# Stick-breaking attention: scores of two heads from half arrays, and the meta tokens' sums over both key blocks at once

## The chip, the cores and the metric

The kernel runs as one program on one core of a Trainium2 chip. The metric is the device time of one execution in microseconds (us). The median of three runs of the kernel before is 1894.74 us (1891.46 to 1902.87).

## The reference, cut to what matters

The network is one block with sparse attention and a mixture of 32 experts, and a second block with two layers. The change lies in the first layer of the second block, the stick-breaking attention over 272 positions (16 meta tokens, then 256 tokens), 16 heads of 64.

```python
def _sb_block(q_blk, k, v, q_pos):
    ...
    z = jnp.einsum('bhqd,bhkd->bhqk', q_blk, k).astype(jnp.float32) * (SB_HEAD_DIM ** -0.5)
    ...
```

From the scores z (masked to keys before the query) each key gets log sigmoid(z) minus the sum of softplus(z) over the keys that lie between it and the query; the exponential of that is the weight of its value row. So for every query the kernel needs, beside z and softplus(z), running sums of softplus(z) over the keys above each key.

## The kernel before, in words

The first block and the experts take the first 1224 us of the span. Then come the attention of this case (1224 to 1405 us), a dense MLP, a recurrent layer, and a last dense MLP. Dense products are split: each fp32 operand is the sum of a high and a low part, and `mm3` (L290 to L292) issues three products of 272 columns for each 128 x 128 tile of weights. The high part of the weights is cast by ScalarE (L190), the low part subtracted by GpSimd or VectorE (L192).

The attention is laid between the dense products of the query, key and value projections. The heads are taken two at a time, as pair t (0 to 7): the two heads lie on partitions 0 to 63 and 64 to 127 of `qT`, `kT` and `vT`. `sb_steps(t)` gives a list of (step, function); `steps` puts it into a background list, and `fill` runs one entry after every second chunk of a dense product (six products). Pairs come in twos, `PAIR` = 11 entries apart, after each group of three projections. Every engine works off its own instructions in the program's order, so the list is the order on all of them.

For a pair, keys are in three parts: "b" (the second 128 tokens), "a" (the first 128 tokens) and "m" (the 16 meta tokens of both heads, 32 rows). The functions are:

- `meta` (step 0): GpSimd lays the meta tokens' keys and values of both heads into padded tiles `km` and `vm`.
- `scores("b")` and `scores("a")` (steps 2 and 3): both heads' scores by one product over all 128 partitions. This needs queries that are zero outside their head: `qz` holds 2 x 272 columns, and `ev_q` fills it with two GpSimd copies (L1973, L1974) from `qT`. A bf16 product with the identity adds the causal mask (L1857, L1860).
- `soft`, `plus`, `rest`: ScalarE does Abs, Exp, Ln on z and copies z to `w`; VectorE forms softplus `sp`; ScalarE casts its high part `sh`, and VectorE subtracts to get the low part `sl` (L1850).
- `sum_b`, `sum_a`, `sum_m` (steps 7, 9, 11): products with triangles and rows of minus ones give the running sums; `weights` adds them to `w` and takes the exponential.
- `values` (step 13): the product with the values, split into `o_hi` and `o_lo`.

In `sum_m` the meta tokens' sum over all later keys is made of `sh` and `sl` of part "a" (256 columns each) and of the unsplit fp32 softplus of part "b" (128 columns, L1903), for each head apart.

Of the kernel before, what the change touches and what calls it, by code (L numbers as in the profile page):

```python
# [8 lines left out]
F32 = mybir.dt.float32  # L9
F32R = mybir.dt.float32r  # L10
# [4 lines left out]
ALU = mybir.AluOpType  # L15
# [6 lines left out]
META = 16  # L22
NT = META + S
# [220 lines left out]
class Ker:  # L244
# [1544 lines left out]
    def sb_steps(self, t):  # L1789
        nc = self.nc  # L1790
        qz, kT, vT = self.qz[t], self.kT[t], self.vT[t]
        sa = self.sba
        st = {}
# [21 lines left out]
        def bank(x):  # L1815
            shape, p = parts[x]
            z = self.ps_o.tile(shape, F32, name="z" + x, tag="z" + x, bufs=1)
            z = st["z" + x] = z[:p]
            st["f" + x] = z if x == "m" else z.rearrange("p a b -> p (a b)")
            return z  # L1820

        def soft(x):

            shape, p = parts[x]
            z = st["f" + x]
            l = sa.tile([128, z.shape[1]], F32, name="l" + x, tag="l" + x)[:p]
            s = sa.tile([128, z.shape[1]], F32, name="sp" + x, tag="sp" + x)[:p]
# [3 lines left out]
            w = st["w" + x] = sa.tile([128, z.shape[1]], F32, name="w" + x, tag="w" + x, bufs=2)[:p]  # L1831
            if x != "a":
                nc.scalar.copy(out=w, in_=z)
            st["p" + x] = l, s

        def plus(x):

            shape, p = parts[x]
            z, (l, s) = st["f" + x], st["p" + x]
            nc.vector.scalar_tensor_tensor(out=s, in0=z, scalar=0.0, in1=l, op0=ALU.max, op1=ALU.add)  # L1840
            s = st["s" + x] = s if x == "m" else s.rearrange("p (a b) -> p a b", a=2)
            hi = st["h" + x] = sa.tile(shape, F32R, name="sh" + x, tag="sh" + x)[:p]
            nc.scalar.copy(out=hi, in_=s)

        def rest(x):
            shape, p = parts[x]
            lo = st["l" + x] = sa.tile(shape, F32R, name="sl" + x, tag="sl" + x)[:p]
            if x == "a":
                nc.vector.tensor_copy(out=st["wa"], in_=st["fa"])
            nc.vector.tensor_tensor(out=lo, in0=st["s" + x], in1=st["h" + x].bitcast(F32), op=ALU.subtract)  # L1850

        def scores(x):
            mk = self.maskd.unsqueeze(1).to_broadcast([128, 2, 128])
            z = bank(x)
            if x == "b":
                mm(z, lhsT=kT[:, META + 128:NT], rhs=qz[:, :, META + 128:NT], start=True, stop=False)
                mm(z, lhsT=self.identb, rhs=mk, start=False, stop=True)  # L1857
            elif x == "a":
                mm(z, lhsT=kT[:, META:META + 128], rhs=qz[:, :, META:NT], start=True, stop=False)  # L1859
                mm(z[:, :, 0:128], lhsT=self.identb, rhs=mk, start=False, stop=True)  # L1860
            else:
                mm(z, lhsT=st["km"], rhs=self.qT[t], start=True, stop=False)
                mm(z[:, 0:16], lhsT=self.identb[0:32, 0:32], rhs=self.maskm[0:32], start=False, stop=True)
            soft(x)

        def weights(x, sums):

            shape, p = parts[x]
# [4 lines left out]
            st["w" + x] = w if x == "m" else w.rearrange("p (a b) -> p a b", a=2)  # L1873

        def sum_b():
            def sums(c):
                for x in ("hb", "lb"):
                    mm(c[:, 0:256].rearrange("p (a b) -> p a b", a=2), lhsT=self.negtri, rhs=st[x], start=(x == "hb"),
                       stop=(x == "lb"))
                return c[:, 0:256]  # L1880

            weights("b", sums)

        def sum_a():
            def sums(c):
# [5 lines left out]
                return c  # L1891
# [17 lines left out]
        def values():  # L1909
            v, wa, wb, wm = st["v"], st["wa"], st["wb"], st["wm"]  # L1910
            ot = self.ps_m.tile([128, 512], F32, name="ot", tag="ss", bufs=1)[:, 0:NT]
            for a in range(2):
# [10 lines left out]
                (8, lambda: plus("m")), (9, sum_a), (9, lambda: rest("m")), (11, sum_m), (13, values)]  # L1923
# [16 lines left out]
    def post_layer0(self, h):  # L1940
        nc = self.nc
        with ExitStack() as ctx:
# [13 lines left out]
            self.qz, self.kT, self.vT, self.qT = {}, {}, {}, {}  # L1956
# [10 lines left out]
            def ev_q(g):  # L1967
                def evac(m, ps):
                    t = 2 * g + m
                    qz = qzs[t % 4]  # L1970
# [4 lines left out]
                    self.qz[t], self.qT[t] = qz, qT  # L1975
# [295 lines left out]
```

## Time and profile before

| what | value |
|---|---|
| median of three runs | 1894.74 us |
| the profiled execution | 1895.64 us |
| its span on the core | 1893.8 us |
| TensorE busy | 1776.0 us, 94% of the span |
| VectorE, ScalarE, GpSimd busy | 991.1, 632.8, 410.2 us |
| read from memory | 546.83 MB, 289 GB/s over the span |

The span is the time on the core; the execution's own time lies 1.84 us above it. Busy time of TensorE overlaps itself, since products are pipelined: a product of 272 columns is shown as 0.29 us long, and the next one starts 0.125 us after it. So what a product costs is read from one start to the next, not from its length.

### The profile page before, as it was taken

The page shows a single profiled execution, that of the slowest core. Times are in us where ns is not written, and L with a number is a line of the kernel's source. Part 1 is how long each engine was busy: PE and PEld are TensorE (multiplying, and loading weights), DVE is VectorE, ACT ScalarE, POOL GpSimd, SP SyncE. Part 2 cuts the span into 40 slices and gives each one's busy share as a digit, 9 for nine tenths or more (in the row PEclk, how much of TensorE's full clock was granted, in tenths as well). Part 3 has the DMA queues.
Part 4 walks back from the last instruction along what each step waited for, and adds up shares of the span by engine and source line. Part 5 has one row for each costly group of instructions (what it writes and reads, how often), then busy time and mean ns, then how long its engine had stood idle before and what let it go on. Part 6 is the DMA issues. An engine that isn't in the chain of part 4 may idle for free. (4 is left out here: it accounts for less than half of the span.)

```text
span 1893.8 us, 25887 instructions
## 1 busy us (share of the span) xinstructions
PE 1776.0 (94%) x10035; PEld 1107.9 (58%) x10035; DVE 991.1 (52%) x1617; ACT 632.8 (33%) x1110; POOL 410.2 (22%) x269
## 2 busy tenths in 40 slices
PE   3988779999999999999999999799999999889998
PEld 2866643333334343333434333377779999889986
DVE  7686744544444433444443444545566543996622
ACT  3444322111211101121110112346565544756633
POOL 4533310000000000000000000164433344554443
PEclk6999989999999999999999999899999999999999
DMA  9544789999999999999999999552245545346552
GB/s 342 205 149 135 251 326 370 424 425 424 424 425 423 425 425 401 424 424 425 423 426 424 400 424 424 222 175 74 74 134 175 182 157 178 112 128 181 181 188 79
DMA packets 183342, 549.60 MB, mean 290 GB/s; under 512 B 8656, under 2 KB 101968, under 8 KB 150256
## 3 DMA queue, kind: packets, MB, share of 16 engines
q1 hardware_dynamic: 182592, 545.99, 74.5%
q0 software_dynamic: 432, 1.57, 0.3%
q8 instruction: 80, 1.31, 0.3%
q10 hardware_dynamic: 192, 0.35, 0.1%
q14 instruction: 46, 0.38, 0.1%
HBM read 546.83 MB, written 1.05 MB: 289 GB/s over the span
## 5 line engine op out<-in xcount | busy, mean ns | idle before, releaser
L192 POOL TENSOR_TENSOR wsp<-wraw,wsp 128x1024 fp32r<-128x1024 f32 x137 | 337.1, 2465 | 1383.8 <-PE cb L1568 964.6
L190 ACT CAST wsp<-wraw 128x1024 fp32r<-128x1024 f32 x208 | 215.4, 1044 | 108.8 <-PE f L2184 46.9
L290 PE MATMUL dps<-hn_hi,wsp 128*128 128x272 f32 (+1 forms) x816 | 242.8, 297 | 9.5 <-DVE h L1935 4.1
L291 PE MATMUL dps<-hn_lo,wsp 128*128 128x272 f32 (+1 forms) x816 | 237.1, 291 | 4.0 <-DVE hn_lo L1637 4.0
L292 PE MATMUL dps<-hn_hi,wsp 128*128 128x272 f32 (+1 forms) x816 | 237.4, 291 | 0.8 <-DVE wsp L192 0.8
L1572 DVE SCALAR_TENSOR_TENSOR h<-cb,vec,h 128x256 f32<-128x256 f32 x256 | 111.8, 479 | 227.5 <-PE cb L1568 227.5
L1441 PE MATMUL u<-wraw_s,xs 128*64 128x512 f32 x728 | 208.5, 602 | 0.9 <-DVE gl L1471 0.9
L1469 ACT COPY gl<-u 64x512 f32<-64x512 f32 x120 | 66.8, 583 | 418.0 <-PE u L1441 357.0
L1441 PE MATMUL u<-wraw,xs 128*64 128x512 f32 x648 | 195.2, 604 | 0.0
L290 PEld LDWEIGHTS dps<-hn_hi,wsp 128*128 128x128 f32 x816 | 157.4, 193 | 14.7 <-issue 5.8
L1441 PE MATMUL u<-wraw_r,xs 128*64 128x512 f32 x544 | 164.4, 608 | 0.0
L291 PEld LDWEIGHTS dps<-hn_lo,wsp 128*128 128x128 f32 x816 | 157.3, 193 | 5.4 <-DVE hn_lo L1637 4.7
L292 PEld LDWEIGHTS dps<-hn_hi,wsp 128*128 128x128 f32 x816 | 157.3, 193 | 1.1 <-DVE wsp L192 1.1
L1471 DVE TENSOR_TENSOR gl<-u,gl 64x512 f32<-64x512 f32 x120 | 79.1, 680 | 140.9 <-ACT gl L1469 140.9
L192 DVE TENSOR_TENSOR wsp<-wraw,wsp 128x1024 fp32r<-128x1024 f32 x71 | 91.2, 1287 | 90.6 <-ACT wsp L190 90.5
L1441 PEld LDWEIGHTS u<-wraw_s,xs 128*64 128x64 f32 x728 | 54.7, 136 | 75.4 <-issue 66.2
L2035 DVE TENSOR_TENSOR y<-r 128x272 f32<-128x272 f32 (+1 forms) x64 | 53.5, 835 | 62.6 <-ACT r L2032 62.6
L1441 PEld LDWEIGHTS u<-wraw,xs 128*64 128x64 f32 x648 | 49.5, 136 | 60.4 <-issue 51.5
L1543 PE MATMUL y<-wraw_s,at 128*64 128x512 f32 x368 | 82.8, 594 | 0.0
L1543 PE MATMUL y<-wraw_r,at 128*64 128x512 f32 x336 | 78.0, 605 | 3.7 <-SPq L1246 3.7
L1567 PE MATMUL cb<-st,y 128*128 128x256 f32 x256 | 80.2, 336 | 0.1
L1510 ACT COPY at<-at_ps 128x512 f32<-128x512 f32 x34 | 19.9, 587 | 176.9 <-PE at_ps L1508 176.9
(514 smaller groups left out, 3325.4 us busy)
## 6 DMA issues: line engine op xcount, KB each, us to landing
wraw_s<-in_exp_w SPq DMA_DIRECT2D x147, 1024.0 KB, 14.3
wraw_r<-in_exp_w SPq DMA_DIRECT2D x120, 1024.0 KB, 15.4
wraw<-in_exp_w SPq DMA_DIRECT2D x117, 1024.0 KB, 14.1
wraw<-in_mlp_w_up SPq DMA_DIRECT2D x32, 1024.0 KB, 5.4
wraw<-in_mlp_w_down SPq DMA_DIRECT2D x32, 1024.0 KB, 4.8
wraw<-in_ada_w SPq DMA_DIRECT2D x18, 1024.0 KB, 5.9
wraw<-in_sb_w_qkv SPq DMA_DIRECT2D x12, 1024.0 KB, 4.9
wraw<-in_lru_w_in SPq DMA_DIRECT2D x8, 1024.0 KB, 5.0
```

The lines of the kernel that those rows point to most:

```text
L190: nc.scalar.copy(out=hv, in_=src)
L192: e.tensor_tensor(out=lv, in0=src, in1=lr, op=ALU.subtract)
L290: mm(o, lhsT=wh, rhs=xh, start=first, stop=False)
L291: mm(o, lhsT=wh, rhs=xl, start=False, stop=False)
L292: mm(o, lhsT=wl, rhs=xh, start=False, stop=last)
L1441: mm(u[n][64 * j:64 * j + 64], lhsT=xs[:, k, o:o + 64], rhs=w[:, ns], start=(q == 0), stop=(q == 3))
L1469: nc.scalar.copy(out=o, in_=u[n][64:128])
L1471: nc.vector.tensor_tensor(out=o, in0=u[n][R], in1=o, op=ALU.add)
L1543: mm(y[n][64 * j:64 * j + 64], lhsT=at[:, k, 0:64], rhs=w[:, ws], start=(q == 0), stop=(q == 3))
L1567: mm(o, lhsT=yh[:, m * 128:m * 128 + 128], rhs=st, start=True, stop=False)
L1572: nc.vector.scalar_tensor_tensor(out=h[:, m, META:NT], in0=o, scalar=self.mod[:, 40 + m:41 + m], in1=h[:, m, META:NT], op0=ALU.mult, op1=A ...
L2035: nc.vector.tensor_tensor(out=y[:, :n], in0=r[:, :n], in1=r[:, :n], op=ALU.mult)
```

## The change

The padded queries `qz`, their four memsets and the two GpSimd copies per pair go. Scores "b" and "a" are made by two products each, one per head, on 64 of the 128 partitions, straight from `qT` and `kT`. Both parts lie in one tile `z` of two banks, a bank for each head: columns 0 to 255 are part "a", columns 256 to 383 part "b". The mask is added per head. For `sum_m`, GpSimd adds softplus "b" into the later half of softplus "a" (in place, after VectorE has taken `sl` of it), ScalarE casts the result to `ch`, GpSimd subtracts to get `cl`, and the meta tokens' sums take `ch` and `cl` over 256 columns; the fp32 products are gone. The new function `both` stands at step 8, ahead of `plus("m")`.

```diff
         def bank(x):
+            if x == "m":
+                z = self.ps_o.tile([128, NT], F32, name="zm", tag="zm", bufs=1)[:32]
+            else:
+                if x == "b":
+                    st["z"] = self.ps_o.tile([128, 2, 512], F32, name="z", tag="z", bufs=1)
+                z = st["z"][:, :, 0:256] if x == "a" else st["z"][:, :, 256:384]
+            st["f" + x] = z
+            return z
...
         def rest(x):
...
             nc.vector.tensor_tensor(out=lo, in0=st["s" + x], in1=st["h" + x].bitcast(F32), op=ALU.subtract)
+            if x == "a":
+                s = st["sa"]
+                nc.gpsimd.tensor_tensor(out=s[:, :, 128:256], in0=s[:, :, 128:256], in1=st["sb"], op=ALU.add)
+
+        def both():
+            hi, lo = tiles("a", "ch", "cl", dt=F32R)
+            nc.scalar.copy(out=hi, in_=st["sa"])
+            nc.gpsimd.tensor_tensor(out=lo, in0=st["sa"], in1=hi.bitcast(F32), op=ALU.subtract)
+            st["hc"], st["lc"] = hi, lo
...
         def scores(x):
-            mk = self.maskd.unsqueeze(1).to_broadcast([128, 2, 128])
             z = bank(x)
-            if x == "b":
-                mm(z, lhsT=kT[:, META + 128:NT], rhs=qz[:, :, META + 128:NT], start=True, stop=False)
-                mm(z, lhsT=self.identb, rhs=mk, start=False, stop=True)
-            elif x == "a":
-                mm(z, lhsT=kT[:, META:META + 128], rhs=qz[:, :, META:NT], start=True, stop=False)
-                mm(z[:, :, 0:128], lhsT=self.identb, rhs=mk, start=False, stop=True)
+            if x == "m":
...
             else:
+                o = META + 128 if x == "b" else META
+                for a in range(2):
+                    hs = slice(64 * a, 64 * a + 64)
+                    mm(z[:, a], lhsT=kT[hs, o:o + 128], rhs=qT[hs, o:NT], start=True, stop=False)
+                for a in range(2):
+                    mm(z[:, a, 0:128], lhsT=self.identb, rhs=self.maskd, start=False, stop=True)
...
         def sum_m():
...
                 for a in range(2):
                     cs = slice(16 - 16 * a, 48 - 16 * a)
-                    mm(z[:, 16:NT], lhsT=self.negselr[:, cs], rhs=st["ha"][:, a], start=False, stop=False)
-                    mm(z[:, 16:NT], lhsT=self.negselr[:, cs], rhs=st["la"][:, a], start=False, stop=False)
-                    mm(z[:, 144:NT], lhsT=self.c("negsel")[:, cs], rhs=st["sb"][:, a], start=False, stop=False)
+                    for x in ("hc", "lc"):
+                        mm(z[:, 16:NT], lhsT=self.negselr[:, cs], rhs=st[x][:, a], start=False, stop=False)
                 mm(z, lhsT=self.negtrim[0:32], rhs=st["lm"], start=False, stop=True)
...
-                (8, lambda: plus("m")), (9, sum_a), (9, lambda: rest("m")), (11, sum_m), (13, values)]
+                (8, both), (8, lambda: plus("m")), (9, sum_a), (9, lambda: rest("m")), (11, sum_m), (13, values)]
...
-            qzs = [sa.tile([128, 2, NT], F32, name=f"qz{i}") for i in range(4)]
-            for q in qzs:
-                nc.gpsimd.memset(q, 0.0)
...
                     nc.vector.scalar_tensor_tensor(out=qT, in0=ps, scalar=0.125, in1=f["rs"], op0=ALU.mult, op1=ALU.mult)
-                    nc.gpsimd.tensor_copy(out=qz[0:64, 0], in_=qT[0:64])
-                    nc.gpsimd.tensor_copy(out=qz[64:128, 1], in_=qT[64:128])
```

The change moves instructions at three places. The names in square brackets are the semaphores that an instruction waits for; a wait that an earlier instruction of the engine has already made is not repeated.

TensorE, the two score products of a pair (t = 2), before and then in the change; z, za and zb are the scores, dps is a dense product:

```order
L1856 MATMUL zb<-qz_7892,kT 128x256
L1857 LDWEIGHTS identb
L1857 MATMUL zb<-maskd_c,identb 128x256
L290 MATMUL dps<-hn_hi,wsp 128x272
L291 MATMUL dps<-hn_lo,wsp 128x272
L292 MATMUL dps<-hn_hi,wsp 128x272
L290 MATMUL dps<-hn_hi,wsp 128x272
L291 MATMUL dps<-hn_lo,wsp 128x272
L292 MATMUL dps<-hn_hi,wsp 128x272
L1859 MATMUL za<-qz_7892,kT 128x512
L1860 LDWEIGHTS identb
L1860 MATMUL za<-maskd_c,identb 128x2x128
```

```order
L1880 MATMUL z<-maskd_c,identb 128x128
L290 MATMUL dps<-hn_hi,wsp 128x272
L291 MATMUL dps<-hn_lo,wsp 128x272
L292 MATMUL dps<-hn_hi,wsp 128x272
L290 MATMUL dps<-hn_hi,wsp 128x272
L291 MATMUL dps<-hn_lo,wsp 128x272
L292 MATMUL dps<-hn_hi,wsp 128x272
L1878 MATMUL z<-qT,kT 128x256 [waits Activation_49]
L1878 MATMUL z<-qT,kT 128x256
L1880 LDWEIGHTS identb
L1880 MATMUL z<-maskd_c,identb 128x128
```

The six dense products between the two scores are the same; the first product of part "a" (L1878, 128x256) now waits for ScalarE, where L1859 waited for nothing of its own. The ScalarE instruction whose count it waits for is the copy of part "b" out of `z` into `wb`, the fourth of the four that `soft("b")` issues; both parts lie in the same two banks.

TensorE, the meta tokens' sums (t = 2), before and then in the change; sh, sl, ch, cl are the high and low parts:

```order
L1898 MATMUL sum<-shm,negtrim_c 32x272 [waits DVE_49,Activation_49]
L1901 MATMUL sum<-sha,negselr 32x256
L1902 MATMUL sum<-sla,negselr 32x256
L1903 MATMUL sum<-spb,cst 32x128
L1901 MATMUL sum<-sha,negselr 32x256
L1902 MATMUL sum<-sla,negselr 32x256
L1903 MATMUL sum<-spb,cst 32x128
L1904 MATMUL sum<-slm,negtrim_c 32x272 [waits DVE_49]
```

```order
L1913 MATMUL sum<-shm,negtrim_c 32x272 [waits DVE_49,Activation_49]
L1917 MATMUL sum<-cha,negselr 32x256
L1917 MATMUL sum<-cla,negselr 32x256 [waits Pool_49]
L1917 MATMUL sum<-cha,negselr 32x256
L1917 MATMUL sum<-cla,negselr 32x256
L1918 MATMUL sum<-slm,negtrim_c 32x272 [waits DVE_49]
```

The two fp32 products (L1903) are gone, and the third product waits for GpSimd's `cla`.

GpSimd, from the end of `meta` of pair 0 to that of pair 1, before and then in the change; wsp is a low part of weights:

```order
L1804 COPY vm<-vT 64x16
L1973 COPY qz_7892<-qT 64x272 [waits DVE_49]
L1974 COPY qz_7892<-qT 64x272
L192 TENSOR_TENSOR wsp<-wraw,wsp 128x1024 [waits PE_49,Activation_49,Pool_49]
L1973 COPY qz_7893<-qT 64x272 [waits DVE_49]
L1974 COPY qz_7893<-qT 64x272 [waits Pool_49]
L192 TENSOR_TENSOR wsp<-wraw,wsp 128x1024 [waits DMAHW1_49,Activation_49,Pool_49]
L1802 MEMSET km 128x32
```

```order
L1804 COPY vm<-vT 64x16
L192 TENSOR_TENSOR wsp<-wraw,wsp 128x1024 [waits PE_49,Activation_49,Pool_49]
L1861 TENSOR_TENSOR spa<-spa,spb 128x2x128 [waits DVE_49]
L192 TENSOR_TENSOR wsp<-wraw,wsp 128x1024 [waits DMAHW1_49,Activation_49]
L1866 TENSOR_TENSOR cla<-spa,cha 128x512 [waits Activation_49]
L1802 MEMSET km 128x32
```

The copies to `qz` are gone. The addition (L1861) and the subtraction (L1866) stand on either side of a piece of weights (L192); so it is in pairs 0, 2 and 4. In pairs 1, 3, 5, 6 and 7 the subtraction follows the addition at once.

## Rows read from the trace of the kernel before

**Rows 1.** The page, busy tenths of TensorE in 40 slices of 47.3 us.

```profile
PE   3988779999999999999999999799999999889998
```

**Rows 2.** Stages of the window view (engines' busy time, granted clock PEclk, DMA share, GB/s).

```profile
1262.00:1265.00 3.00, 3.00 (x12) 1.87 (x11) 0.46 (x1) 1.68 (x4) 2.09 (x1) 0.50 0.00 0
1280.00:1320.00 40.00, 37.64 (x254) 30.58 (x254) 21.05 (x39) 24.29 (x51) 20.20 (x23) 1.00 0.20 67
1406.00:1408.00 2.00, 2.00 (x11) 2.00 (x10) 1.99 (x6) 1.73 (x4) 0.00 (x0) 0.50 0.96 264
```

**Rows 3.** TensorE's waits from 1250 to 1410 us: total, times, longest.

```profile
PE vtr L1810 <- POOL vm L1804: 3.2, 1, 3.2
PE dps L290 <- DVE h L1935: 2.8, 2, 2.1
PE sum L1878 <- DVE slb L1850: 2.8, 2, 1.4
PE sum L1904 <- DVE slm L1850: 1.6, 2, 0.8
```

**Rows 4.** Timeline, the scores of pair 2 (start, length, engine, line).

```profile
1291.93 0.59 PE L1856 MATMUL zb<-qz,kT 128*128 128x256 f32 x2
1292.36 0.27 PE L1857 MATMUL zb<-maskd_c,identb 128*128 128x256 bf16 x1
1293.22 1.02 PE L1859 MATMUL za<-qz,kT 128*128 128x512 f32 x2
1293.86 0.35 ACT L1833 COPY wb<-zb 128x256 f32<-128x256 f32 x1
1294.08 0.27 PE L1860 MATMUL za<-maskd_c,identb 128*128 128x256 bf16 x1
```

**Rows 5.** Timeline, scores of two heads in the first block.

```profile
134.44 0.93 PE L834 MATMUL sc<-z 64*128 64x128 f32 x8
135.29 0.39 PE L290 MATMUL dps<-hh,wsp 128*128 128x256 f32 x1
```

**Rows 6.** Timeline, part "a" and the meta tokens' sums of pair 7.

```profile
1386.60 0.68 DVE L1850 TENSOR_TENSOR sla<-spa,sha 128x512 fp32r<-128x512 f32 x1
...
1389.27 0.31 PE L1898 MATMUL sum<-shm,negtrim_c 32*32 32x272 f32 x1
1389.50 0.31 PE L1901 MATMUL sum<-sha,negselr 128*32 128x256 f32 x1
1389.65 0.28 PE L1902 MATMUL sum<-sla,negselr 128*32 128x256 f32 x1
1389.86 0.41 PE L1903 MATMUL sum<-spb,cst 128*32 128x128 f32 x2
...
1390.88 0.31 PE L1904 MATMUL sum<-slm,negtrim_c 32*32 32x272 f32 x1
```

**Rows 7.** Timeline, the same place in pair 2.

```profile
1300.66 0.62 ACT L1843 CAST sha<-spa 128x512 fp32r<-128x512 f32 x1 [3.10 <-DVE spa L1840]
...
1301.48 0.68 DVE L1850 TENSOR_TENSOR sla<-spa,sha 128x512 fp32r<-128x512 f32 x1
...
1302.99 1.04 ACT L190 CAST wsp<-wraw 128x1024 fp32r<-128x1024 f32 x1
...
1304.16 2.36 POOL L192 TENSOR_TENSOR wsp<-wraw,wsp 128x1024 fp32r<-128x1024 f32 x1 [0.71 <-POOL qz L1974]
...
1304.38 2.43 DVE L1850 TENSOR_TENSOR slm<-spm,shm 32x272 fp32r<-32x272 f32 x1 [0.56 <-ACT shm L1843]
...
1306.87 0.31 PE L1904 MATMUL sum<-slm,negtrim_c 32*32 32x272 f32 x1 [0.79 <-DVE slm L1850]
```

**Rows 8.** Timeline, GpSimd and ScalarE ahead of pair 0.

```profile
1231.15 0.85 POOL L1656 TENSOR_TENSOR sq<-sq 128x272 f32<-128x272 f32 x1
...
1244.97 1.99 ACT L190 CAST wsp<-wraw 128x1024 fp32r<-128x1024 f32 x2
...
1247.56 11.76 POOL L192 TENSOR_TENSOR wsp<-wraw,wsp 128x1024 fp32r<-128x1024 f32 x5
```

More of the change, by code (lines that the diff above doesn't have):

```diff
@@ L1790, in sb_steps @@
         nc = self.nc
-        qz, kT, vT = self.qz[t], self.kT[t], self.vT[t]
+        qT, kT, vT = self.qT[t], self.kT[t], self.vT[t]
         sa = self.sba
@@ L1815, in bank, with tiles @@
         def bank(x):
+            if x == "m":
[6 more added lines that the diff above has]
+            return z
+        def tiles(x, *names, dt=F32, **kw):
             shape, p = parts[x]
[L1817 to L1820, printed above, removed]
+            return [sa.tile(shape, dt, name=n + x, tag=n + x, **kw)[:p] for n in names]
         def soft(x):
-            shape, p = parts[x]
             z = st["f" + x]
-            l = sa.tile([128, z.shape[1]], F32, name="l" + x, tag="l" + x)[:p]
-            s = sa.tile([128, z.shape[1]], F32, name="sp" + x, tag="sp" + x)[:p]
+            l, s = tiles(x, "l", "sp")
             nc.scalar.activation(out=l, in_=z, func=AF.Abs)
@@ L1830, in soft @@
             nc.scalar.activation(out=l, in_=l, func=AF.Ln, bias=1.0)
-            w = st["w" + x] = sa.tile([128, z.shape[1]], F32, name="w" + x, tag="w" + x, bufs=2)[:p]
+            w, = tiles(x, "w", bufs=2)
+            st["w" + x] = w
             if x != "a":
@@ L1836, in plus @@
         def plus(x):
-            shape, p = parts[x]
             z, (l, s) = st["f" + x], st["p" + x]
             nc.vector.scalar_tensor_tensor(out=s, in0=z, scalar=0.0, in1=l, op0=ALU.max, op1=ALU.add)
-            s = st["s" + x] = s if x == "m" else s.rearrange("p (a b) -> p a b", a=2)
-            hi = st["h" + x] = sa.tile(shape, F32R, name="sh" + x, tag="sh" + x)[:p]
+            st["s" + x] = s
+            hi, = tiles(x, "sh", dt=F32R)
+            st["h" + x] = hi
             nc.scalar.copy(out=hi, in_=s)
         def rest(x):
-            shape, p = parts[x]
-            lo = st["l" + x] = sa.tile(shape, F32R, name="sl" + x, tag="sl" + x)[:p]
+            lo, = tiles(x, "sl", dt=F32R)
+            st["l" + x] = lo
             if x == "a":
@@ L1850, in rest @@
             nc.vector.tensor_tensor(out=lo, in0=st["s" + x], in1=st["h" + x].bitcast(F32), op=ALU.subtract)
+            if x == "a":
[6 more added lines that the diff above has]
+            st["hc"], st["lc"] = hi, lo
         def scores(x):
[L1853 removed]
             z = bank(x)
[L1855 to L1863 removed]
+            if x == "m":
+                mm(z, lhsT=st["km"], rhs=qT, start=True, stop=False)
+                mm(z[:, 0:16], lhsT=self.identb[0:32, 0:32], rhs=self.maskm[0:32], start=False, stop=True)
+            else:
+                o = META + 128 if x == "b" else META
[4 more added lines that the diff above has]
+                    mm(z[:, a, 0:128], lhsT=self.identb, rhs=self.maskd, start=False, stop=True)
             soft(x)
         def weights(x, sums):
[L1868 removed]
             c = sums(self.ps_o.tile([128, 512], F32, name="sum", tag="sum", bufs=1))
@@ L1872, in weights @@
             nc.scalar.activation(out=w, in_=w, func=AF.Exp)
-            st["w" + x] = w if x == "m" else w.rearrange("p (a b) -> p a b", a=2)
         def sum_b():
             def sums(c):
+                z = c[:, 0:256].rearrange("p (a b) -> p a b", a=2)
                 for x in ("hb", "lb"):
-                    mm(c[:, 0:256].rearrange("p (a b) -> p a b", a=2), lhsT=self.negtri, rhs=st[x], start=(x == "hb"),
-                       stop=(x == "lb"))
-                return c[:, 0:256]
+                    mm(z, lhsT=self.negtri, rhs=st[x], start=(x == "hb"), stop=(x == "lb"))
+                return z
             weights("b", sums)
@@ L1890, in sums @@
                 mm(z, lhsT=self.negtri, rhs=st["la"], start=False, stop=True)
-                return c
+                return z
             weights("a", sums)
```

5 lines of the change are left out of this document (2 added, 3 removed).

## The prediction

> **What bounds the kernel now.** I read the busy tenths first, then the stages, TensorE's waits, and the timeline of two pairs of heads. TensorE is the engine to follow: from the attention on (slice 27) its tenths are 8 or 9 [rows 1], and the products of the layers behind stand in one line on it, so I let a delay of the attention pass to the end in full. The attention runs from 1254 to 1405 us. Between 1280 and 1320 us TensorE is busy for 37.64 of 40 us at a clock of 1.00 [rows 2]: there are few gaps, and they are named. Between 1250 and 1410 us TensorE waits once for `vm` (3.2 us, pair 0), and in pairs 2 and 4 for `slb` (1.4 us each) and `slm` (0.8 us each) [rows 3]. In pairs 1, 3, 5, 6 and 7 it waits for nothing of the attention; there a product saved is time saved, and a wait added is time lost. After its two longest pauses, 3.2 and 2.1 us [rows 3], its granted clock is 0.50, the level of 1.2 GHz; the first such stretch lasts 3.0 us [rows 2]. Half the work of 3.0 us is lost in it, 1.5 us.
>
> **The scores.** Today part "b" takes 0.43 us (1291.93 to 1292.36) and part "a" 0.86 us (1293.22 to 1294.08), together 1.29 us [rows 4]. The change needs the same columns from half arrays. The first block has just this pattern: L834 makes 128 and 256 columns for two heads on either half, each head in a bank of its own, and takes 0.85 us from its start to the next product [rows 5]. The ends are 0.65 us (both heads wholly side by side) and 1.29 us (one after the other); 0.85 us is the same shape, so I take it: 0.44 us saved per pair, 0.29 of it in part "a". The Trainium skill (TensorEngine Tiling, Theoretical Speedup) allows up to 2x for 64 rows, which would be the 0.65 us and take 1.6 us off the sum; L834 shows less than that, and its row goes into the sum. The mask becomes two products with a load of the identity each. A switch that shows a load costs 0.08 us more than one that hides it (0.23 against 0.15 between the first three products of [rows 6]); two more switches are 0 to 0.16 us, and I take 0.1.
>
> **The new wait in the scores.** The order shows the first product of part "a" waiting for ScalarE's copy `wb`. In pair 2 that copy ends at 1293.86 + 0.35 = 1294.21, while part "a" started at 1293.22 [rows 4]: 0.99 us. In the other seven pairs the same difference is 0.98 to 0.99. A shorter part "b" brings both sides forward alike. So each pair pays 0.99 us, behind which all later dense products of TensorE queue. Today TensorE writes `za` while ScalarE reads `zb` [rows 4], in separate tiles, at no cost; no row shows two engines in one bank. The Trainium skill (PSUM — Partial Sum Buffer, Terms) calls two engines on one bank and quadrant at the same time an error, reads included. By that rule the wait has to stay; without it the sum would be 7.9 us lower.
>
> **The meta tokens' sums.** In pair 7 they take 1389.27 to 1390.88, 1.61 us from first to last start [rows 6]. Without the two fp32 products there remain 0.23 + 3 x 0.15 + 0.23 = 0.91 us by the steps in the same rows: 0.70 us saved per pair.
>
> **The new wait in the sums.** The third product now needs a chain: VectorE's `sla`, GpSimd's addition, ScalarE's cast, GpSimd's subtraction. GpSimd takes 0.85 us for 272 columns and 2.36 us for 1024 [rows 7, 8]; on the line between them 256 columns take 0.81 us and 512 take 1.33. By share of the long piece alone they would take 0.59 and 1.18; held up by a VectorE row of the size of `slm` (0.42) more. The cast is 0.62 us [rows 7].
>
> - Pairs 1, 3, 5, 6, 7. The chain starts later by the wait less the shorter part "a" and some 0.05 for the mask: 0.99 - 0.29 + 0.05 = 0.75. In pair 7 `sla` ends at 1387.28 [rows 6], so `cl` is there at 1387.28 + 0.75 + 0.81 + 0.62 + 1.33 = 1390.79. TensorE would reach that product at 1389.27 + 0.38 + 0.65 = 1390.30, the 0.65 being 0.99 - 0.44 + 0.1. It waits 0.49. Net per pair: 0.65 - 0.70 + 0.49 = +0.44; five pairs, **+2.2 us**.
> - Pairs 2 and 4. A piece of weights stands between addition and subtraction. In pair 2 its cast ends at 1304.03, GpSimd starts it at 1304.16 and holds it 2.36 us [rows 7]. Shifted by 0.75, it ends at 1307.27, the subtraction at 1308.6, and the last product of the sums starts 0.53 later, at 1309.13, against 1306.87 today [rows 7]. **+2.26 us each, +4.5.** TensorE sits idle some 2.3 us at the third product, since `shm`, now behind the new cast, is ready at about 1305.9.
> - Pair 0. Without the copies to `qz`, GpSimd can start its five pieces when the first cast is done, near 1246.0 and not at 1247.56 [rows 8], so `vm` comes 1.5 us sooner and the wait of 3.2 falls to about 1.1; the half clock after it, 1.5 us, goes. Its sums lose 0.70 and gain the 2.3 us wait: -1.5 - 1.5 - 0.7 + 2.3 = **-1.4 us**.
>
> **The clock.** The new pauses of 2.3 us in pairs 0, 2 and 4 are nearest to the one of 2.1 us that was followed by 0.50 [rows 2, 3]; pauses of 1.4 and 0.8 us in pair 2 were not (clock 1.00, [rows 2]). I take 1.5 us for each of the three, **+4.5 us**; the ends are none and all eight pairs (12 us).
>
> **Sum.** 2.2 + 4.5 - 1.4 + 4.5 = +9.8 us. The profiled execution took 1895.64 us (span 1893.8 and 1.84 around it), 0.9 above the median of 1894.74; on the median the forecast is 1904.5 us. VectorE's queue is not charged: in pairs like 7 `slm` is held until the subtraction ends and is done within 0.5 us after it, as TensorE reaches its last product; GpSimd's pieces of weights that follow start up to 2.1 us later, in front of which lie pieces split ahead. If that cover is gone, a dense product waits for it, at most 2.1 us per pair.
>
> **Rivals.**
>
> 1. *The saved products decide: faster.* Both waits are covered, because ScalarE's and GpSimd's chains run ahead of TensorE. Then each pair gains 0.44 - 0.1 + 0.70 = 1.04, eight pairs 8.3, and pair 0 its 3.0: -11.3, 1883 us. For it: five pairs wait for nothing today. Against it: the copy would have to end 0.99 us sooner, before TensorE arrives; that is the point from which it decides, and nothing removed shortens the four ScalarE instructions ahead of it. Chance 0.10.
> 2. *The halves run one after the other.* Then 0.44 per pair is not saved, +3.5, and part "a" delays the chain by 0.29 more in pairs that wait: about 1908 to 1910. Against it stands L834. Chance 0.12.
> 3. *The clock falls in every pair.* Five more times 1.5: 1912; with late pieces of weights up to 1920. For it: the gaps of a pair now lie close together. Against it: the longest single pause in pairs 1, 3, 5, 6, 7 is 1.0. Chance 0.08.
> 4. *Savings and waits cancel; the change shows nothing.* GpSimd at its fastest (0.37 less per pair, 3.0) and no fall of the clock (4.5): 9.8 - 7.5 = +2.3, and with the halves wholly side by side +0.7: 1895 to 1897. Chance 0.15.
>
> The forecast as worked out, waits that outweigh the savings with the clock falling in some pairs (1898 to 1908), has 0.55. The range that should hold the time 8 times in 10 is 1893 to 1912: it takes in rivals 2 and 4, most of the forecast's bounds, the edge of rival 3, and leaves out rival 1. About 1% (19 us) is what a measurement of this kernel can tell from no change. Faster by that would need more than all savings, 0.02; slower by it only rival 3 with the halves in series, 0.07; within it 0.91.
>
> **What the profile will show.** If I am right: the scores of part "a" (L1878) wait about 1 us for `wb` in all eight pairs; L1917 waits for GpSimd, 2 us and more in pairs 0, 2, 4 and about 0.5 in the rest; the wait for `vm` is about 1 us; the four score products cost 0.85 us in sum; the stretches of 0.50 follow the long pauses. I am wrong if TensorE's waits in the attention do not grow, if L1917 finds `cl` ready, or if the waits are there and the layers behind start no later.

## The result: 0.7% slower, where 0.5% slower was forecast

| kernel | median | executions |
|---|---|---|
| before | 1894.24 us | 10 |
| changed | 1908.95 us | 10 |

The changed kernel takes 1.0072 times as long, with a 95% interval of 1.0054 to 1.0091: 14.7 us more by the medians. The forecast was 1904.5 us in a range of 1893 to 1912, with 0.91 on "within 1%". The sign, the range and "within 1%" hold; the size was 4.5 us short.

Single executions of one kernel lie up to 14 us apart (before: 1890 to 1904 us in later rounds). A part of that stands ahead of the attention: the last start of L1746 lies between 1240.3 and 1251.6 us in the traces of the kernels below. So times are compared by medians, and places by the length of one stage inside a trace. The stage used below runs from the last start of L1746 (the dense products that open the attention) to the first start of the MLP's Relu. Before it is 1243.2 to 1410.2, 167.0 us. In the changed kernel it is 1242.6 to 1424.4, 181.8 us. The stage is 14.8 us longer, about the difference of the medians; that the two agree so well is in part chance (see the part on why the prediction was right). Each such length comes from one profiled execution.

### The profile after

The page of the changed kernel, TensorE's busy tenths and the granted clock in 40 slices, answers to [rows 1]:

```profile
PE   3988779999999999999999999788899999889998
PEclk7999979999999999999999999898999999989999
```

Slices 27 to 29 (47.7 us each) now read 8, 8, 8, and the clock reads 8 in slice 28 (1288 to 1336 us), the part of pairs 2 and 3. TensorE's waits between 1250 and 1425 us (total, times, longest) answer to [rows 3]:

```profile
PE sum L1917 <- POOL km L1802: 7.8, 4, 2.5
PE z L1878 <- ACT wb L1840: 6.6, 8, 0.8
PE sum L1894 <- DVE slb L1857: 3.1, 3, 1.3
PE dps L290 <- DVE h L1949: 2.8, 2, 2.1
PE sum L1913 <- ACT shm L1850: 2.1, 3, 0.7
PE sum L1917 <- POOL cla L1866: 1.4, 4, 0.4
PE vtr L1810 <- POOL vm L1804: 0.7, 1, 0.7
```

Both waits that were forecast are there. L1878 waits for the copy `wb` in all eight pairs, 0.81 to 0.83 us each. L1917 waits for GpSimd in all eight, 2.46 to 2.47 us in pairs 0, 2 and 4. (The view names `km` in four of them, because that is the next instruction of GpSimd's queue; the timeline below shows that `cla` ends there.) The wait for `vm` fell from 3.2 to 0.7 us. The waits rose from 10.8 [rows 3, and 0.4 for `shm`] to 24.5 us.

The timeline of pair 7, which no half clock touches, answers to [rows 4] and [rows 6] (start, length, engine, line, operation):

```profile
1392.47 0.49 PE L1878 MATMUL z<-qT,kT 64*128 64x128 f32 x4
1392.90 0.29 PE L1880 MATMUL z<-maskd_c,identb 128*128 128x128 bf16 x2
...
1394.40 0.35 ACT L1840 COPY wb<-z 128x256 f32<-128x256 f32 x1
...
1394.81 0.70 PE L1878 MATMUL z<-qT,kT 64*128 64x256 f32 x4 [0.82 <-ACT wb L1840]
1395.45 0.28 PE L1880 MATMUL z<-maskd_c,identb 128*128 128x128 bf16 x2
...
1403.90 0.31 PE L1913 MATMUL sum<-shm,negtrim_c 32*32 32x272 f32 x1
1404.13 0.31 PE L1917 MATMUL sum<-cha,negselr 128*32 128x256 f32 x1
1404.78 0.30 PE L1917 MATMUL sum<-cla,negselr 128*32 128x256 f32 x1 [0.34 <-POOL cla L1866]
...
1405.25 0.31 PE L1918 MATMUL sum<-slm,negtrim_c 32*32 32x272 f32 x1
```

Before, the scores of the same pair were these:

```profile
1378.63 0.70 PE L1856 MATMUL zb<-qz,kT 128*128 128x256 f32 x2
1379.17 0.27 PE L1857 MATMUL zb<-maskd_c,identb 128*128 128x256 bf16 x1
1380.04 1.02 PE L1859 MATMUL za<-qz,kT 128*128 128x512 f32 x2
```

Part "b" takes 0.43 us from its start to the mask (1392.47 to 1392.90). Before it took 0.43 in the even pairs [rows 4] and 0.54 in the odd ones, as here in pair 7. Part "a" takes 0.64 (1394.81 to 1395.45), against 0.86. From the mask of "b" to the start of "a" it is 1.91 us (before: 0.87). The view puts 0.82 of that down as idle, since it counts from the end of the product before; from start to start the wait costs 0.98, with 0.06 for the second mask product. The sums take 1.35 us from first to last start, against 1.61. Their wait is 0.34 of idle time and 0.50 from start to start (0.65 between `cha` and `cla`, less the 0.15 of such a step without a wait).

The timeline of pair 2 answers to [rows 7]:

```profile
1305.02 0.74 POOL L1861 TENSOR_TENSOR spa<-spa,spb 128x256 f32<-128x256 f32 x1 [2.49 <-DVE sla L1857]
...
1305.77 1.03 ACT L190 CAST wsp<-wraw 128x1024 fp32r<-128x1024 f32 x1
...
1306.71 0.61 ACT L1865 CAST cha<-spa 128x512 fp32r<-128x512 f32 x1
1306.88 2.35 POOL L192 TENSOR_TENSOR wsp<-wraw,wsp 128x1024 fp32r<-128x1024 f32 x1 [1.12 <-ACT wsp L190]
...
1309.19 1.45 POOL L1866 TENSOR_TENSOR cla<-spa,cha 128x512 fp32r<-128x512 f32 x1
...
1310.70 0.42 PE L1917 MATMUL sum<-cla,negselr 128*32 128x256 f32 x1 [2.47 <-POOL km L1802]
```

This is the forecast order: addition, cast, a piece of weights of 2.35 us on GpSimd, and only then the subtraction, whose end at 1310.64 releases TensorE. The product after it lasts 0.42 us and not 0.31: the clock has fallen. The windows of two such stretches (busy time of TensorE, granted clock, DMA share, GB/s) answer to [rows 2]:

```profile
1309.00:1317.00 8.00, 6.30 (x28) 0.57 0.01 2
1319.00:1323.00 4.00, 3.64 (x17) 0.57 0.06 23
```

The first is pair 2 and lasts twice as long as in pairs 0 and 4. The second is pair 3, where no pause is longer than 0.82 us.

### The profile page after: what moved, and what is told of

It reads as the page before. It is cut to its first block, busy times and chain, and to the rows that moved or that the text cites. A ratio compares the mean times of both kernels' runs of the same rounds, so it can differ in the third digit from the quotient of the medians.

```text
span 1908.3 us, 25912 instructions
## 1 busy us (share of the span) xinstructions
PE 1778.0 (93%) x10051; PEld 1113.6 (58%) x10051; DVE 996.5 (52%) x1617; ACT 634.9 (33%) x1118; POOL 419.3 (22%) x265
## 5 line engine op out<-in xcount | busy, mean ns | idle before, releaser
L192 POOL TENSOR_TENSOR wsp<-wraw,wsp 128x1024 fp32r<-128x1024 f32 x137 | 337.9, 2471 | 1376.0 <-PE cb L1568 962.3
L192 DVE TENSOR_TENSOR wsp<-wraw,wsp 128x1024 fp32r<-128x1024 f32 x71 | 90.8, 1282 | 91.4 <-ACT wsp L190 90.0
L1567 PEld LDWEIGHTS cb<-st,y 128*128 128x128 f32 x256 | 48.4, 189 | 52.0 <-issue 41.9
## 6 DMA issues: line engine op xcount, KB each, us to landing
wraw_r<-in_exp_w SPq DMA_DIRECT2D x120, 1024.0 KB, 14.9
```

What stands on the lines that cost most here:

```text
L192: e.tensor_tensor(out=lv, in0=src, in1=lr, op=ALU.subtract)
L1567: mm(o, lhsT=yh[:, m * 128:m * 128 + 128], rhs=st, start=True, stop=False)
```

## Experiments

Each was timed in rounds beside the kernel before, whose median was 1894.25, 1894.32 and 1893.76 us in the three groups. Kernels of different groups, the changed one among them, are set against each other through that kernel.

| kernel | median | ratio to before, 95% interval | stage |
|---|---|---|---|
| before | 1894.24 | | 167.0 |
| changed | 1908.95 | 1.0072 (1.0054 to 1.0091) | 181.8 |
| new scores alone | 1897.78 | 1.0008 (0.9991 to 1.0025) | 171.6 |
| new sums alone | 1903.10 | 1.0036 (1.0018 to 1.0054) | 176.8 |
| scores back to back | 1901.90 | 1.0034 (1.0018 to 1.0051) | 174.8 |
| subtraction on VectorE | 1918.29 | 1.0111 (1.0083 to 1.0138) | 191.5 |
| pauses filled | 1903.78 | 1.0045 (1.0028 to 1.0062) | 175.4 |
| chain one step earlier | 1894.14 | 0.9998 (0.9980 to 1.0015) | 170.1 |
| new scores alone, back to back | 1896.96 | 1.0008 (0.9990 to 1.0027) | 168.2 |
| back to back, unsplit sum | 1893.74 | 0.9996 (0.9977 to 1.0014) | 166.4 |
| new sums alone, chain earlier | **1889.88** | **0.9967 (0.9951 to 0.9982)** | 163.6 |
| back to back, chain earlier | 1892.36 | 0.9992 (0.9977 to 1.0007) | 164.4 |
| new sums alone, unsplit | 1891.49 | 0.9981 (0.9968 to 0.9994) | 164.6 |
| back to back, unsplit, filled | 1893.72 | 1.0009 (0.9993 to 1.0025) | 167.6 |

The ratio is not the quotient of the two medians; the two differ by up to 0.0016. Differences in us below are of medians, unless they are said to be of the stage.

The theory: the loss is made of the wait for `wb`, the wait for `cla` behind a piece of weights, and the half clock after it. The rivals: the loss lies in the products themselves, in late weights, or in ScalarE.

### 1. Each half of the change alone

New scores alone (against the changed kernel; the addition on GpSimd goes as well, and lines are left out at the dots):

```diff
-                    for x in ("hc", "lc"):
-                        mm(z[:, 16:NT], lhsT=self.negselr[:, cs], rhs=st[x][:, a], ...)
+                    ... the three products of before, from ha, la and sb
-                (8, both), (8, lambda: plus("m")), ...
+                (8, lambda: plus("m")), ...
```

> The change's scores (half arrays, shared two banks, no padded queries) with the meta tokens' sums of before. Theory (waits and the clock): part "a" still waits 0.8 us for the copy of part "b" in eight pairs, 6.6 us; the score products save 1.29 - 1.05 = 0.24 us a pair, 1.9; pair 0 keeps the 3.0 us from the earlier vm and the clock. No wait at the meta tokens' sums, no half clock in pairs 2 and 4: +2 us against before (1 to 5), so most of the 14 us is gone. Rival 1 (products on half arrays cost more on TensorE than the trace shows): +8 us or more. Rival 2 (all comes from GpSimd holding VectorE): about -3 us.

New sums alone (against the kernel before; `both` as in the change, lines left out at the dots):

```diff
+            if x == "a":
+                s = st["sa"]
+                nc.gpsimd.tensor_tensor(out=s[:, :, 128:256], in0=s[:, :, 128:256], in1=st["sb"], op=ALU.add)
-                    ... the three products from ha, la and sb
+                    for x in ("hc", "lc"):
+                        mm(z[:, 16:NT], lhsT=self.negselr[:, cs], rhs=st[x][:, a], start=False, stop=False)
-                (8, lambda: plus("m")), ...
+                (8, both), (8, lambda: plus("m")), ...
```

> The kernel before with only the new meta tokens' sums (addition and subtraction on GpSimd); padded queries stay. Theory (waits and the clock): in pairs 0, 2, 4 the third product waits some 2 us for the subtraction and the clock falls to 0.50 behind each such pause; in the other five the wait of 0.4 us is less than the 0.70 saved: +6 us against before (4 to 10). Rival 1 (half arrays are the cost): -3 us. Rival 2 (GpSimd holds VectorE): +10 or more, with VectorE's slb and slm as the longest waits of TensorE rather than cla.

Measured: 3.5 us over before with the scores alone (its interval includes 1), 8.9 with the sums alone. The first of these two fences is the scores alone, the second the sums alone (TensorE's waits, as above):

```profile
PE z L1874 <- ACT wb L1840: 6.6, 8, 0.8
...
```

```profile
PE sum L1913 <- POOL km L1802: 8.0, 3, 3.0
PE vtr L1810 <- POOL vm L1804: 3.1, 1, 3.1
...
```

In the trace of the scores alone no pair shows a stretch of 0.50, and the wait for `wb` is there in full. In that of the sums alone pairs 0, 2 and 4 do, and the wait of 3.1 us for `vm` stays, since the copies to `qz` stay. The stages are 4.6 and 9.8 us longer than before; together that is 14.4 of the 14.8. So by the stages the halves add, and the sums are two thirds of the loss. By the medians they come to 12.4 of 14.7, where each interval is some 3 us wide to either side.

### 2. The wait for the copy

Scores back to back: both parts' products are issued at step 2, ahead of the first reader of their banks (`False` leaves out the softening that `scores` ends with; that line of the edit is not shown).

```diff
+        def scores_ba():
+            scores("b", False)
+            scores("a", False)
+            soft("b")
...
-                (2, lambda: scores("b")), (3, lambda: scores("a")), ...
+                (2, scores_ba), (3, lambda: soft("a")), ...
```

> The change with the products of part "b" and part "a" issued back to back at step 2, ahead of ScalarE's first reading of the two banks. Theory: the wait of part "a" (0.82 us x 8) is gone, ScalarE's chain for part "a" starts a little sooner, the waits for cla and the half clock stay: 5 to 7 us faster than the change. Rival (the wait only stands in for one that comes later, since ScalarE's chain sets the pace): within 2 us of the change.

The time fell by 7.1 us. The wait for `wb` is gone and that for `cla` stays (7.1 us). The same edit with the old sums came later:

> The kernel before with only the new scores, and the products of parts b and a issued back to back ahead of the mask's reader, so that part a waits for no copy; the meta tokens' sums are those of before. Theory (the wait for the copy of wb, 0.83 us in each of 8 pairs, ate the 0.24 us per pair that the halves save and more): the wait is 0, the time lies 4 to 8 us below the kernel with the new scores alone (1897.8), at 1890 to 1894, 0 to 4 us below the kernel before. Rival (the softening of part b comes later for it and slb and slm are waited for instead): 1896 to 1899 us.

It gave 0.9 us against the scores alone, and the rival's range held. TensorE's waits in it:

```profile
PE sum L1896 <- DVE slb L1857: 4.2, 3, 2.0
...
PE vtr L1810 <- POOL vm L1804: 1.7, 1, 1.7
PE sum L1907 <- DVE sla L1857: 1.4, 3, 0.5
...
```

The 6.6 us for `wb` are gone, but `slb` costs 4.2 and not 3.1, `vm` 1.7 and not 0.7, and `sla` 1.4 and not 0: 3.5 of the 6.6 come back, because the softening of part "b" now starts behind part "a". The rest, 3.1 us, shows in the stage (171.6 to 168.2) and not in the median. With the new sums the edit gave 7 us in both. In that trace three stretches of 0.50, all of the single length, follow waits of 2.5 us (pairs 0 and 2) and 2.0 us (pair 4), and pair 3 has none. TensorE's waits in the view fell from 24.5 to 19.9 us, and the time at a granted clock of 0.50 from 17 to 10 us, of which half, at most 3.5 us, is lost work. Together that is enough for the 7 us; the scores alone had no such stretch that could go. But whether the clock makes the difference was not tried by itself.

### 3. Where the subtraction stands

Subtraction on VectorE:

```diff
-            nc.gpsimd.tensor_tensor(out=lo, in0=st["sa"], in1=hi.bitcast(F32), op=ALU.subtract)
+            nc.vector.tensor_tensor(out=lo, in0=st["sa"], in1=hi.bitcast(F32), op=ALU.subtract)
```

> The change with the subtraction that makes cl on VectorE (some 0.68 us there) and not on GpSimd, so that no piece of weights stands ahead of it. Theory: the pauses of 2.5 us in pairs 0, 2, 4 shrink under 1 us and the clock stays at 1.00 there: 10 to 13 us faster than the change, near the time of before. Rival (the pauses are not what sets the time; VectorE's chain is): under 5 us faster, since VectorE gets 0.68 us more per pair.

This missed on the wrong side: 9.3 us slower than the changed kernel. Timeline of pair 0:

```profile
1266.18 2.34 POOL L192 TENSOR_TENSOR wsp<-wraw,wsp 128x1024 fp32r<-128x1024 f32 x1 [1.13 <-ACT wsp L190]
1266.65 2.41 DVE L1866 TENSOR_TENSOR cla<-spa,cha 128x512 fp32r<-128x512 f32 x1 [2.06 <-ACT cha L1865]
...
1268.99 0.42 DVE L1846 SCALAR_TENSOR_TENSOR spm<-zm,lm 32x272 f32<-32x272 f32 x1
...
1269.44 0.42 ACT L1850 CAST shm<-spm 32x272 fp32r<-32x272 f32 x1 [2.83 <-DVE spm L1846]
...
1270.15 0.40 PE L1913 MATMUL sum<-shm,negtrim_c 32*32 32x272 f32 x1 [3.85 <-DVE wa L1887]
```

The same operation on 128x512 (`sla`) takes VectorE 0.68 us [rows 6]. Here it lasts 2.41 us and ends 0.54 us after GpSimd's piece, and `spm`, `shm` and TensorE's first product of the sums stand behind it: 3.85 us, against 0.69 in the changed kernel. The Trainium skill (SBUF — State Buffer, Who interferes with whom) says that a VectorE instruction with two inputs in SBUF contends with a GpSimd instruction that reads SBUF; this trace agrees, with 2.41 us for work of 0.68. So moving the subtraction off GpSimd does not take it from behind the piece of weights. Nor is that all: in the other five pairs it lasts 0.69 us, and TensorE's first product of the sums still waits 1.2 to 1.6 us, since VectorE stands idle for the cast `cha` (1.2 to 1.6 us) with `spm` behind it in its queue.

Chain one step earlier, in the changed kernel:

```diff
-                (7, lambda: rest("a")), (8, both), (8, lambda: plus("m")), ...
+                (7, lambda: rest("a")), (7, both), (8, lambda: plus("m")), ...
```

> The changed kernel with the chain for the meta sums (addition, cast, subtraction) moved one step earlier in the list of parts, so that GpSimd makes addition and subtraction ahead of the piece of weights in all pairs, and ScalarE the cast ahead of its piece. Theory (the piece of 2.35 us between addition and subtraction makes the pauses of 2.47 us in pairs 0, 2, 4, and these make the half clock): the wait at the third product is at most 0.5 us in all pairs, no stretch of 0.50 in pairs 0, 2, 4, time 10 to 13 us below the changed kernel, 1896 to 1899 us. Rival (the weights come late instead: dps waits for h 2 us more in those pairs, and the clock falls there): 3 to 6 us below the changed kernel.

It fell by 14.9 us, to the time of the kernel before: a little more than the theory's 10 to 13. Timeline of pair 2, and TensorE's waits:

```profile
1300.00 0.73 POOL L1861 TENSOR_TENSOR spa<-spa,spb 128x256 f32<-128x256 f32 x1 [2.49 <-DVE sla L1857]
1301.46 1.27 POOL L1866 TENSOR_TENSOR cla<-spa,cha 128x512 fp32r<-128x512 f32 x1 [0.73 <-ACT cha L1865]
1302.69 2.68 POOL L192 TENSOR_TENSOR wsp<-wraw,wsp 128x1024 fp32r<-128x1024 f32 x1
```

```profile
PE z L1878 <- ACT wb L1840: 6.6, 8, 0.8
...
PE sum L1917 <- POOL cla L1866: 1.3, 4, 0.3
...
PE sum L1917 <- POOL km L1802: 0.4, 1, 0.4
```

The piece now stands behind the subtraction, the wait for `cla` is 0.4 us or less, and no dense product waits for the weights that come later: of the 9.2 us at L1917 1.7 are left. No stretch of 0.50 is left in pairs 0, 2 and 4, as expected. But the clock still falls twice, though no pause is left that is long: in the scores of pair 1 and of pair 3, each time right behind the wait for `wb`. The window of pair 1 (its part "a" starts at 1271.66 us), the timeline of pair 3's scores, and its window:

```profile
1272.00:1275.00 3.00, 3.00 (x16) 0.50 0.83 263
```

```profile
1309.36 1.13 PE L1878 MATMUL z<-qT,kT 64*128 64x256 f32 x4 [0.82 <-ACT wb L1840]
...
1310.42 0.40 PE L1880 MATMUL z<-maskd_c,identb 128*128 128x128 bf16 x2
```

```profile
1309.00:1313.00 4.00, 3.64 (x17) 0.57 0.42 131
```

The product of part "a" takes 1.06 us from start to mask there, against 0.64 in pair 7 above. So a pause of 0.82 us can stand ahead of a stretch of 0.50, as in pair 3 of the changed kernel; in the other six pairs the same pause was not followed by one.

### 4. The clock by itself

Pauses filled: 18 products that nothing reads, where TensorE stood idle in pairs 0, 2 and 4.

```diff
                     for x in ("hc", "lc"):
+                        if a == 0 and x == "lc" and t in (0, 2, 4):
+                            d = self.ps_o.tile([128, 512], F32, name="vtr", tag="vtr", bufs=1)
+                            for _ in range(18):
+                                mm(d[:, 0:256], lhsT=self.negtri, rhs=st["ha"][:, 0], start=True, stop=True)
                         mm(z[:, 16:NT], lhsT=self.negselr[:, cs], rhs=st[x][:, a], start=False, stop=False)
```

> The changed kernel with 18 extra products of 256 columns (into a bank that nothing reads, about 0.11 us each, 2 us in sum) on TensorE ahead of the third product of sum_m in pairs 0, 2 and 4, where it stood idle for 2.47 us. Nothing else is changed. Theory (the pause itself lets the granted clock fall, and half of the work after it is lost): the pause shrinks to about 0.5 us, no stretch of 0.50 follows in pairs 0, 2, 4, and the time falls by 5 to 7 us, to 1902 to 1904 us beside 1909 of the changed kernel. Rival (the clock falls for another reason, as the smaller work of the whole pair, or the loss in these pairs lies in the dense products waiting for weights): stretches of 0.50 stay, time within 1.5 us of the changed kernel or above it.

The time fell by 5.2 us (stage: 6.4), though the kernel does 54 products more. Two windows, first of the changed kernel and then of this one, each from the attention's start to short of its end:

```profile
1243.00:1415.00 172.00, 148.94 (x1005) 0.95 0.27 89
```

```profile
1251.00:1420.00 169.00, 150.61 (x1071) 1.00 0.28 90
```

The mean granted clock is 1.00 instead of 0.95, in pair 3 too. Just behind its window, from 1421 to 1425 us, this kernel has a stretch of 0.50 (0.57 on the mean) that the changed kernel does not have, so the time falls by less than the stage. So the half clock in the attention costs 5 to 6 us of the 14.7, and filling idle TensorE takes it away; the waits cost the rest.

### 5. Versions that keep what was good

> The scores of before, with the new meta tokens' sums whose chain is moved one step earlier (addition, cast and subtraction ahead of GpSimd's piece of weights). Theory (the sums over both blocks save 0.70 us per pair as soon as their chain is done in time): the wait at the third product is at most 0.5 us, the kernel lies 4 to 8 us below the changed kernel with the chain moved (1894.1), since it has no wait for the copy of wb, and 2 to 5 us below the kernel before: 1887 to 1892 us. Rival (the saved products are used up by the small waits that remain): 1893 to 1896 us, no difference to before.

The edit is that of the chain one step earlier, made in "new sums alone". It is the fastest kernel here: 3.9 us below before by the medians, with an interval (0.9951 to 0.9982) that leaves out 1. TensorE's waits:

```profile
PE vtr L1810 <- POOL vm L1804: 3.1, 1, 3.1
...
PE sum L1889 <- DVE slb L1850: 2.8, 2, 1.4
PE sum L1909 <- ACT shm L1843: 2.2, 3, 0.7
PE sum L1913 <- POOL cla L1860: 1.4, 4, 0.3
PE sum L1913 <- POOL km L1802: 0.4, 1, 0.4
```

Against before the wait for `slm` (1.6) is gone, those for `shm` and `cla` came (1.8 each), and the sums have two fp32 products of 128 columns fewer per pair. The new scores cost 3.7 us on top of it (0.2 below before against 3.9 below).

Scores back to back (experiment 2) and the chain one step earlier (experiment 3), both in the changed kernel:

> The changed kernel with both moves: the score products of parts b and a back to back, and the chain for the meta sums one step earlier. Theory (the two waits are the whole of the loss, and their removals add up): -7 and -15 us against the changed kernel together, less 3 to 5 that both count as clock loss in pair 2: 1889 to 1893 us. Rival (back to back, slb comes 0.6 us later for the sums of part b, as in the two kernels with this move so far, so nothing is gained over the chain alone): 1893 to 1896 us.

At 1892.36 us the theory's range held, but the interval includes 1, and without the new scores it is 2.5 us less: back to back they still earn nothing.

The next two take the cast and the second subtraction away and use GpSimd's fp32 sum as it is:

```diff
-                    for x in ("hc", "lc"):
-                        mm(z[:, 16:NT], lhsT=self.negselr[:, cs], rhs=st[x][:, a], start=False, stop=False)
+                    mm(z[:, 16:NT], lhsT=self.c("negsel")[:, cs], rhs=st["sa"][:, a], start=False, stop=False)
-                (8, both), (8, lambda: plus("m")), ...
+                (8, lambda: plus("m")), ...
```

First in the kernel with scores back to back, then in "new sums alone":

> The same scores back to back, and the meta tokens' sums over both blocks from the sum that GpSimd makes in fp32: one fp32 product of 256 columns in place of two float32r ones, without the cast on ScalarE and the second subtraction on GpSimd. Theory (cast and subtraction, 0.62 and 1.45 us and the piece of weights between, make the wait at the third product; the addition alone is done in time): no wait above 0.5 us for GpSimd there, no half clock in pairs 2 and 4, 1888 to 1894 us. Rival (the addition is late as well, or its one fp32 product costs what the three before cost): 1896 to 1902 us.

> The scores of before, and the meta tokens' sums over both blocks from the fp32 sum that GpSimd makes, unsplit: one fp32 product of 256 columns per head, no cast and no second subtraction. Theory: the addition is done in time in all pairs, ScalarE and GpSimd have less to do than with the split sum; 1888 to 1893 us, the same as or 1 to 2 us above the split sum with its chain moved. Rival (fp32 products run at a quarter of the rate and cost 0.4 us each): 1894 to 1898 us.

With scores back to back it gave 1893.74 us, within the theory's range, but not for all its reasons: the clock falls in two pairs, behind waits of 2.0 us for `slb`. With the old scores it gave 1891.49, faster than before by 0.06 to 0.32%. It comes within 2 us of the split sum with the chain earlier, and needs no chain.

The last fills a pause in the first of these two:

```diff
                 z = c[:, 0:256].rearrange("p (a b) -> p a b", a=2)
+                if t in (2, 4):
+                    for _ in range(16):
+                        mm(c[:, 0:128], lhsT=self.negtri, rhs=self.negtri, start=True, stop=True)
                 for x in ("hb", "lb"):
```

> The kernel with score products back to back and unsplit sum (1893.7 us), with 16 extra products of 128 columns (into the bank that the sums then overwrite) ahead of the sums of part b in pairs 2 and 4, where TensorE stood idle for 2.0 us for slb. Theory (idle TensorE lets the clock fall and 3 us are lost in these two pairs): no stretch of 0.50 in pairs 2 and 4, 2 to 4 us below: 1890 to 1892 us. Rival (the extra products last longer than the wait, or the clock falls all the same): 1893 to 1896 us.

Here the rival held. The wait for `slb` fell to 0.3 us at most, but that for `slm` rose from 1.1 us in one pair to 3.3 us in three, and a stretch of 0.50 is left in the attention. Filling a pause saves only where no other chain is late behind it.

## Why the prediction was right, and where it was short

**What bounds the kernel.** Right: the products behind the attention stand in line on TensorE, and its delay reaches the end. That stage (14.8) and time (14.7) agree is in part luck. By TensorE's own starts, counted from the last start of L1746, the first dense product behind pair 7's sums comes 15.0 us later (1391.12 before, 1405.49). Then 1.4 us come back: before, the pause of 2.1 us for `h` was followed by 0.50 [rows 2], and in the changed kernel the same pause is not. Timeline and window there:

```profile
1419.86 0.36 PE L290 MATMUL dps<-hn_hi,wsp 128*128 128x272 f32 x1 [2.11 <-DVE h L1949]
```

```profile
1420.00:1423.00 3.00, 3.00 (x25) 1.00 0.92 276
```

So the product of L1675 behind it is 13.5 us late (1410.77 before, 1423.71). The stage does not show this, because the Relu that ends it waits for ScalarE, which has casts ahead of it. Another 1.5 us are added in the last layers, where the trace of the changed kernel has a stretch of 0.50 (1722 to 1726 us) that the one before lacks. The forecast had neither.

**The scores.** The direction was right, the size not: 1.07 us for both parts (0.43 and 0.64) where 0.85 was taken from [rows 5], so 0.22 saved in the even pairs and 0.33 in the odd ones, instead of 0.44. In [rows 5] the products of two heads come as one run of eight; here each part is cut by its mask. That this makes the difference is likely, but no run shows it. The Trainium skill's "up to 2x" (TensorEngine Tiling, Theoretical Speedup) is met by neither part: 1.0 to 1.26 times for "b" and 1.34 for "a".

**The wait for `wb`.** Right in place, number (all eight pairs) and size: 0.98 us from start to start in pair 7, where 0.99 was forecast. The 0.82 of the view is a shorter measure of the same wait.

**The sums.** Right: in pair 7 they are 0.26 us shorter with their wait (1.35 against 1.61), where 0.70 saved and 0.49 waited, 0.21 shorter, was forecast. The starts of pair 7's first and last product lie 0.53 further apart (12.78 against 12.25, before's first product starting at 1378.63); forecast was 0.44. Measured from one copy of `wb` to the next, pairs 1, 5 and 6 grew by 0.71, 0.69 and 0.6. So the excess in these pairs comes from the scores.

**Pairs 2 and 4.** The 2.26 us per pair were right, for the reason given. From the first score product to the last product of the sums it was 14.94 us in both (in pair 2 1291.93 to 1306.87). In the changed kernel the third product of the sums starts 16.82 us after pair 2's first (1293.88 to 1310.70), and three steps at full clock, 0.47 us as in pair 7, make 17.29: 2.35 later. Pair 4 gives the same.

**Pair 0.** The forecast was -1.4, and +0.1 with the clock; it measured +1.74. The scores and the shorter wait for `vm` came to -1.46 us (forecast -1.5), and the half clock behind it went (-1.3). But TensorE, coming sooner, then met two chains that had been covered: `slb` for 0.43 us and `shm` for 0.69 us (idle time; from start to start `slb` costs 0.58). The sums grew by 2.7 us with `shm`, where 2.3 - 0.7 = 1.6 was forecast. The step that failed is "the wait goes" without what is late next.

**The clock.** This is the term that was mis-sized most. The forecast had three stretches of 1.5 us in pairs 0, 2 and 4. They came, but the stretch of pair 2 lasted 7 us (about 2.25 us lost: 4.6 measured less 2.35), and one more followed a pause of 0.82 us in pair 3 (about 1.55 lost: 2.2 less 0.65). That pauses of 0.8 us "were not" followed by 0.50 was read from one trace; the changed kernel and the chain one step earlier show the contrary. And that a pause of 2.1 us is followed by it was read from one place; in the changed kernel it is not.

Pair by pair the excess over the forecast is 1.6 (pair 0), 0.85 (pair 2), 1.75 (pair 3) and 0.7 (the other five): 4.9 us; the 1.4 us that came back behind the attention and the 1.5 us added later cancel. **Of the rivals**, the second named the time (1908 to 1910), yet its mechanism gives only 1.3 us: halves that save 0.22 rather than 0.44 in four pairs, and 0.33 in the other four. That the time fell into its range is chance. Rival 1 (the saved products decide) became true in sign, though only for 3.9 of its 11.3 us, in another order, in the new sums alone with the chain one step earlier.

What stays open: why the clock fell in pair 3 and not behind the same pause in pairs 5 to 7, and why taking the wait for `wb` away beside the old sums shortened the stage by 3.4 us and the median by 0.9.

## What to carry to other kernels

A chain over two engines that replaces products on the busy engine is worth what its slowest place in the queues makes of it: the same addition, cast and subtraction cost 9 us with a long piece of other work between them and gained 4 us ahead of it. Before two tiles are put into one bank, look for the reader of the first that the writer of the second will meet. Price a wait from one start to the next, as products are, and not by the idle time of the view. When a wait goes, ask in the same step which chain is next; and give the clock a price for every added pause, also short ones, as a range.

## What the runs showed of the hardware

- Two products on 64 rows each, in banks of their own, took 0.22 us less than the 0.86 of 128 rows at 256 columns per head; at 128 columns per head they took 0.43 us, where 128 rows took 0.43 in the even pairs and 0.54 in the odd ones.
- A VectorE subtraction of 0.68 us lasted 2.41 us beside a GpSimd subtraction of 2.34 us.
- Products that nothing reads, put into idle time of TensorE, made the kernel 5.2 us faster, with a mean granted clock of 1.00 instead of 0.95 in the attention.
- A pause of TensorE of 2.1 us was followed by a granted clock of 0.50 in the kernel before and not in the changed one; one of 0.82 us was followed by it in two of eight pairs with the chain one step earlier.
